# Dealing pooling out ahead of the projection of retention's q and k between the steps of attention

## The chip, the cores and the metric

The kernel runs on one core of a Trainium2 chip. The metric is the device time of one execution in microseconds (us). Engines are named as the profile names them: PE multiplies matrices, ACT applies functions and copies, DVE works elementwise, POOL and SP mainly issue transfers here.

## What is computed

A backbone of two layers over 256 noisy tokens `x` and 256 context tokens `ctx`, width 1024, in fp32. Each layer mixes tokens by three parallel groups of heads that share one input and one output projection, and then applies a channel mixer (a dense SwiGLU in layer 0, the best 2 of 8 experts in layer 1). Only `x` is returned, so layer 1 needs the context only as keys and values.

```python
def token_mixers(hx, hc, w_in, w_out, ...):
    aqx, akx, avx, rqx, rkx, rvx, rgx, ppx = _split_projection(hx @ w_in)
    aqc, akc, avc, rqc, rkc, rvc, rgc, ppc = _split_projection(hc @ w_in)
    ...
    attn_x = _merge_attn(_blocked_attention(qx, k_all, v_all))       # softmax attention, 8 heads
    ...
    ret_x = _ret_output(ret_x, rgx)                                  # retention, 4 heads: rq, rk, rv, gate rg
    pool_x = multiscale_pool(ppx, pool_w, pool_scale)                # means over windows of pp, then pool_w
    mx = jnp.concatenate([attn_x.astype(hx.dtype), ret_x.astype(hx.dtype), pool_x], axis=-1) @ w_out
```

Retention needs rq and rk of the input projection (called q/k below); pooling needs only pp.

## The kernel before

**Products.** An fp32 product is made of three matmuls of rounded parts (`mm3`, L231 to L233: high by high, high by low, low by high). `split` (L161, L162) makes the parts: ACT copies the high part, DVE subtracts it to get the low one. Weights come in blocks of 1 MB through a ring of four (`wload`, L169) and are split the same way. Normalised tokens stand in `hh` and `hl` (`features`), one buffer each.

**PSUM.** Three kinds of buffers: four named `mm` for projections, three named `at` for attention and retention, one named `md`.

**Attention.** `attend` goes over pairs of heads and, within a head, over tiles of 128 queries: four tiles in layer 0 (two of `x` against 512 keys, two of `ctx` against 256), two in layer 1. A tile takes an `at` buffer for its scores (L720, two matmuls), DVE finds the negated maximum (L723), ACT takes the exponential with its sum (L726), DVE inverts and scales (L727, L728), PE transposes (L731, into the same buffer) and ACT copies to SBUF (L734). Only then is the buffer free. After the two heads of a pair, L743 multiplies by the values into another `at` buffer, and that is split into `mixa`. The steps are 4 to prepare and 32 tiles in layer 0, 4 and 16 in layer 1.

**Side work.** `weave` deals out steps of a second generator between the steps of attention, 0.55 of a step for each in layer 0 and one in layer 1. The second generator is a chain: `values` (the projection of retention's v), `gp` (of its gate and of pooling's input), `project_qk` (of its q and k: 32 products of three matmuls, with 512 columns in layer 0 and 256 or 512 in layer 1), and `pool_tokens`. What is left when attention is through its steps is emitted behind it by `finish`.

`project_qk` ends with conversions: POOL clears (L769), ACT copies (L770 to L772) and DVE subtracts (L777). They write into the one buffer of `hh` and `hl` that the projection's matmuls read, so they start only behind the last of those. `pool_tokens` multiplies by the table `band` (L817, 8 matmuls for each of two steps), copies (L821, ACT), multiplies by the pooling weights (L823), scales (L826, DVE) and splits (L161, L162).

**Order.** The program order is not yet that of the engines: a scheduler orders the instructions of each engine from the program order, data dependences and free buffers. The order is fixed when the kernel is built, and each engine keeps to its own.

**Behind it.** `retain` takes scores (L895, from the conversions), masks them (L897) and multiplies by v (L917). The output projection multiplies `w_out` by `mixa`, retention's `mr` and pooling's `mp`, with four `mm` buffers for its sums. In layer 0 POOL also loads the residual (L847).

Of the kernel before, what the change touches and what calls it, by code (L numbers as in the profile page):

```python
# [86 lines left out]
def weave(main, side, ratio):  # L87

    due = 0.0
    for _ in main:  # L90
        due += ratio
        while due >= 1:
            due -= 1
            next(side, None)


class Net:
# [36 lines left out]
    def s2(self, shape, name, dt=F32):  # L134
        return self.tmp.tile(shape, dt, name=name, tag="s2", bufs=5)
# [439 lines left out]
    def mixer(self, l, pool, xin=None):  # L575
# [17 lines left out]
        def tok(cols, n, tiles, evac, ahead=None, tail=1):  # L593

            out = {t: self.mm() for t in tiles}

            def op(o, t, k, wh, wl, start, stop):
                s = slice(t * 128, t * 128 + 128)
                self.mm3(o[:, :n], (hh[:, k, s], hl[:, k, s]), (wh, wl), start, stop)

            yield from self.product(self.units(I["w_in"][l, cols // 256:(cols + n) // 256], n, pace=rate * 512 // n, ahead=ahead), out, op, tail)
            for t in tiles:
                evac(t, out[t])
# [149 lines left out]
        def project_qk():  # L753
            out = {b: self.mm() for b in range(4)}

            def op_qk(o, b, k, wh, wl, start, stop):
                n = QN if b < 2 else 512
                s = slice(b * 128, b * 128 + 128)
                self.mm3(o[:, :n], (wh[:, s], wl[:, s]), (hh[:, k, :n], hl[:, k, :n]), start, stop)

            yield from self.product(self.units(I["w_in"][l, 3:5], 512, pace=rate), out, op_qk, 1)
            qq, kk = self.features()
            qd, qz, kp = qq[:, 0:4, :QN], qq[:, 4:8, :QN], kk[:, 0:4]
            ret.update(qd=qd, qz=qz, kp=kp, kk=kk)
            parts = []
            for hd in range(4):
                i, j = slice(64 * (hd % 2), 64 * (hd % 2) + 64), slice(64 - 64 * (hd % 2), 128 - 64 * (hd % 2))
                q, k = out[hd // 2][i, :QN], out[2 + hd // 2][i]
                nc.gpsimd.memset(qz[j, hd].bitcast(F32), 0.0)  # L769
                nc.scalar.activation(qd[i, hd], q, AF.Copy)  # L770
                nc.scalar.activation(qd[j, hd], q, AF.Copy)
                nc.scalar.activation(kp[i, hd], k, AF.Copy)  # L772
                parts.append((qz[i, hd], q, qd[i, hd]))
                parts.append((kp[j, hd], k, kp[i, hd]))
                if hd % 2:
                    for lo, x, hi in parts:
                        v.tensor_sub(lo, x, hi.bitcast(F32))  # L777
                    parts = []
# [11 lines left out]
        def values():  # L790
            yield from tok(1280, 256, (0, 1, 2, 3), lambda t, p: nc.scalar.activation(rv[:, t], p[:, :256], AF.Copy))

            r3 = rv.rearrange("p t (h d) -> p (t h) d", d=64)
            mu = self.small.tile([128, 16], F32, name="mu", tag="mu", bufs=1)
            v.tensor_reduce(mu, r3, axis=AX.X, op=OP.add)
            v.tensor_scalar(mu, mu, 1.0 / 64, None, op0=OP.mult)
            v.tensor_tensor(r3, r3, mu[:, :, None].to_broadcast([128, 16, 64]), op=OP.subtract)


        def pool_tokens():  # L800
            band, ys = [], []
            for m in range(2):
                t = pool.tile([128, 4, 256], F32, name="band", tag="band", bufs=2)
                nc.sync.dma_start(t, I["band"][:, m * 1024:(m + 1) * 1024].rearrange("p (g t) -> p g t", g=4))
                band.append(t)
            wp = pool.tile([128, 2, 128], F32, name="wp")
            v.memset(wp, 0.0)
            for g in range(4):
                i = 64 * (g % 2)
                nc.gpsimd.dma_start(wp[i:i + 64, g // 2, i:i + 64], I["pool_w"][l, g])  # L810
            for pr in range(2):
                p = self.mm()
                for side in range(QN // 256):
                    for m in range(2):
                        for i in range(2):
                            g = 2 * pr + i
                            nc.tensor.matmul(p[64 * i:64 * i + 64, side * 256:side * 256 + 256],  # L817
                                             lhsT=pp[:, 2 * side + m, g * 64:g * 64 + 64], rhs=band[m][:, g],
                                             start=m == 0, stop=m == 1, tile_position=(0, 64 * i))
                mx = s2([128, 512], "mixed")  # L820
                nc.scalar.activation(mx[:, :QN], p[:, :QN], AF.Copy)  # L821
                p2 = self.mm()
                nc.tensor.matmul(p2[:, :QN], lhsT=wp[:, pr], rhs=mx[:, :QN], start=True, stop=True)  # L823
                y = s2([128, 512], "pooled")
                c = 32 + 2 * l + pr
                v.tensor_scalar(y[:, :QN], p2[:, :QN], self.fcol[:, c:c + 1], None, op0=OP.mult)  # L826
                ys.append(y)
                yield
            mp.extend(pool.tile([128, 2, QN], F32R, name="mp", tag="band", bufs=2) for _ in range(2))
            for pr in range(2):  # L830
                self.split(mp[0][:, pr], mp[1][:, pr], ys[pr][:, :QN])

        mr, mp = [], []
        gp = tok(1536, 512, QT, ev_gp)
        side = chain(*(values(), gp, project_qk(), pool_tokens()))
        weave(attend(), side, 0.55 if need else 1.0)
        finish(side)
        self.mid = self.latest(DVE, ACT)
# [126 lines left out]
        if need:  # L965
            side = self.product(self.units(w[0:2], 512, back=True, pace=1), outs, op_out, 1)
        else:
            side = self.product(self.units(w, 1024, pace=1, order=(0, 2, 6, 4)), outs, op_out, 2)
# [786 lines left out]
```

## Time and profile before

| | |
|---|---|
| median of 3 runs | 1526.49 us (1525.47 to 1529.04) |
| the profiled execution | 1525.96 us, of which 1523.7 us are the span |
| mean granted clock of PE | 0.982 |
| PE | 1453.4 us busy, 95% of the span |
| DVE, ACT | 823.5 us (54%), 617.2 us (41%) |
| POOL | 61.0 us (4%) |
| transfers | 410.82 MB, mean 270 GB/s |

The profile shows one execution. The span runs from the first to the last instruction; 2.3 us of the execution's time lie outside it. Attention's last tiles and the start of the output projection stand at about 185 to 201 us in layer 0 and at 736 to 747 us in layer 1. In each row of a timeline stand the start, the duration, the engine, the line, the output and the inputs, and in brackets how long the engine had been idle and what released it. Matmuls overlap in the pipeline, so durations of neighbours overlap too, and a row of the trace may count one matmul of 64 rows twice.

### The profile page before, as it was taken

What the parts mean: (1) busy time and instruction counts of PE and PEld (TensorE: products, weight loads), DVE (VectorE), ACT (ScalarE), POOL (GpSimd) and SP (SyncE); (2) the same over time, 40 slices, a digit from 0 to 9 for tenths busy, and PEclk for the clock granted to TensorE, in tenths of its full rate; (3) what the DMA queues carried; (4) which work ended last, traced back from release to release, by engine and by line L of the source; (5) the groups of instructions that cost most, each with busy time, mean ns of one, the idle gap of its engine ahead of it and who ended that gap; (6) DMA issues with size and microseconds to landing.
All of it is one profiled execution on the core that took longest, in us unless ns stands there. A gap on an engine that the chain in (4) does not pass through costs nothing. (4 is left out here: it accounts for less than half of the span.)

```text
span 1523.7 us, 22762 instructions
## 1 busy us (share of the span) xinstructions
PE 1453.4 (95%) x9006; PEld 1053.9 (69%) x9007; DVE 823.5 (54%) x1557; ACT 617.2 (41%) x983; POOL 61.0 (4%) x96
## 2 busy tenths in 40 slices
PE   7999999999999999999999999999999899999796
PEld 5777667988878888787666478755786476774462
DVE  3496687774555544877763089515982143533112
ACT  4337654423222222456642177414771243433111
POOL 1010200000000001000000000000001000000000
PEclk9999999999999999999999999999999999999998
DMA  9773223353453625352367999999999999899983
GB/s 348 276 285 138 90 93 138 125 210 122 165 198 123 219 92 199 126 175 91 139 235 310 420 410 420 420 420 420 408 420 414 408 420 408 333 335 349 376 351 158
DMA packets 63044, 410.82 MB, mean 270 GB/s; under 512 B 9477, under 2 KB 10185, under 8 KB 15697
## 3 DMA queue, kind: packets, MB, share of 16 engines
q1 hardware_dynamic: 54864, 392.19, 65.6%
q0 software_dynamic: 5664, 16.29, 3.0%
q8 instruction: 73, 1.20, 0.3%
q10 hardware_dynamic: 2400, 0.79, 0.2%
q14 instruction: 43, 0.34, 0.1%
HBM read 402.27 MB, written 6.98 MB: 269 GB/s over the span
## 5 line engine op out<-in xcount | busy, mean ns | idle before, releaser
L162 DVE TENSOR_TENSOR wl<-w,wh 128x1024 fp32r<-128x1024 f32 x310 | 374.6, 1223 | 256.9 <-ACT wh L161 247.4
L161 ACT ACTIVATE wh<-w 128x1024 fp32r<-128x1024 f32 x310 | 324.0, 1059 | 369.7 <-PE at L233 113.1
L1339 PE MATMUL mm<-w,few 128*64 128x256 f32 (+2 forms) x2624 | 235.0, 346 | 0.0
L1339 PEld LDWEIGHTS mm<-w,few 128*64 128x64 f32 (+1 forms) x2624 | 153.4, 132 | 72.1 <-issue 17.1
L1368 PE MATMUL mm<-w,few 128*64 128x512 f32 (+1 forms) x616 | 111.2, 536 | 0.0
L231 PE MATMUL mm<-hh,wh 128*128 128x512 f32 (+1 forms) x256 | 95.7, 374 | 1.2 <-ACT hh L161 1.2
L232 PE MATMUL mm<-hl,wh 128*128 128x512 f32 (+1 forms) x256 | 95.7, 374 | 0.0
L233 PE MATMUL mm<-hh,wl 128*128 128x512 f32 (+1 forms) x256 | 95.4, 373 | 0.0
L1303 DVE TENSOR_TENSOR mg<-mg,mm 128x256 f32<-128x256 f32 (+2 forms) x36 | 13.6, 378 | 133.7 <-ACT mg L1302 133.7
L1368 PEld LDWEIGHTS mm<-w,few 128*64 128x64 f32 (+1 forms) x616 | 34.9, 129 | 70.7 <-issue 68.9
L233 PE MATMUL mm<-wh,hl 128*128 128x256 f32 (+1 forms) x240 | 80.8, 342 | 0.0
L232 PE MATMUL mm<-wl,hh 128*128 128x256 f32 (+1 forms) x224 | 75.4, 339 | 1.8 <-DVE wl L162 1.8
L231 PE MATMUL mm<-wh,hh 128*128 128x256 f32 (+1 forms) x224 | 75.1, 340 | 0.0
L1302 ACT ACTIVATE mg<-mm 128x256 f32<-128x256 f32 (+3 forms) x54 | 22.8, 422 | 122.2 <-PE mm L1339 84.1
L363 DVE SCALAR_TENSOR_TENSOR wsum<-w,sc,wsum 128x1024 f32<-128x1024 f32 x48 | 59.6, 1280 | 22.9 <-DMA w<-in_w_mod_dram 22.8
L232 PE MATMUL at<-hl,wh 128*128 128x512 f32 (+1 forms) x192 | 71.3, 371 | 0.0
L233 PE MATMUL at<-hh,wl 128*128 128x512 f32 (+1 forms) x192 | 71.3, 371 | 0.0
L231 PE MATMUL at<-hh,wh 128*128 128x512 f32 (+1 forms) x192 | 71.3, 371 | 0.0
L231 PE MATMUL mm<-wh,xh 128*128 128x512 f32 (+1 forms) x144 | 57.9, 402 | 7.5 <-ACT wh L161 7.5
L232 PE MATMUL mm<-wl,xh 128*128 128x512 f32 (+1 forms) x144 | 57.1, 396 | 2.6 <-DVE wl L162 2.6
L231 PEld LDWEIGHTS mm<-hh,wh 128*128 128x128 f32 x256 | 48.2, 188 | 11.2 <-issue 2.1
L233 PE MATMUL mm<-wh,xl 128*128 128x512 f32 (+1 forms) x144 | 55.7, 387 | 0.0
(486 smaller groups left out, 2589.5 us busy)
## 6 DMA issues: line engine op xcount, KB each, us to landing
w<-in_moe_w_dram SPq DMA_DIRECT2D x264, 1024.0 KB, 14.9
w<-in_w_mod_dram SPq DMA_DIRECT2D x48, 1024.0 KB, 4.9
w<-in_ffn_w_dram SPq DMA_DIRECT2D x33, 1024.0 KB, 4.9
w<-in_w_in_dram SPq DMA_DIRECT2D x16, 1024.0 KB, 5.1
w<-in_w_out_dram SPq DMA_DIRECT2D x8, 1024.0 KB, 4.8
gate<-gscr POOLq DMA_DIRECT2D x5, 512.0 KB, 4.6
band<-in_band_dram SPq DMA_DIRECT2D x4, 512.0 KB, 7.4
yrows<-zero POOLq DMA_DIRECT2D x4, 512.0 KB, 7.8
```

The source lines that it names most:

```text
L161: self.nc.scalar.activation(hi, x, AF.Copy)
L162: self.nc.vector.tensor_sub(lo, x, hi.bitcast(F32))
L231: mm(out, lhsT=a[0], rhs=b[0], start=start, stop=False)
L232: mm(out, lhsT=a[0], rhs=b[1], start=False, stop=False)
L233: mm(out, lhsT=a[1], rhs=b[0], start=False, stop=stop)
L363: nc.vector.scalar_tensor_tensor(x, y, c, x, op0=OP.mult, op1=OP.add)
L1302: nc.scalar.activation(s1[:r, :c], h1[:r, :c], AF.Silu)
L1303: v.tensor_mul(s1[:r, :c], s1[:r, :c], h3[:r, :c])
L1339: nc.tensor.matmul(h[i][m * j:m * j + m, :c], lhsT=x[0][:, k], rhs=t[:, k - k0, j * c:j * c + c], start=k == 0, stop=k == KB - 1, tile_pos ...
L1368: nc.tensor.matmul(y[0][m * q:m * q + m, :c], lhsT=x[0][:, b], rhs=w[:, j, c * q:c * q + c], start=f + j == 0, stop=f + j == FB - 1, tile_ ...
```

## The change

In the chain of side work, `pool_tokens` stands ahead of `project_qk`. Nothing is added or removed.

```diff
         gp = tok(1536, 512, QT, ev_gp)
-        side = chain(*(values(), gp, project_qk(), pool_tokens()))
+        side = chain(*(values(), gp, pool_tokens(), project_qk()))
         weave(attend(), side, 0.55 if need else 1.0)
         finish(side)
```

PE, layer 0, behind the last products of `gp` (the first row below, at about 129 us in the trace before); rows with - are of the kernel before, rows with + of the changed one. `mm<-hh,wh` and its like are products of q/k, `mm<-band,pp` pooling, `at` attention.

```order
 L233 MATMUL mm<-wh,hl 128x512
-L231 MATMUL mm<-hh,wh 128x512
+L817 MATMUL mm<-band,pp 64x256
 L731 MATMUL at<-cst,pe 128x128 x8
 L720 MATMUL at<-kT,qT 128x256 x2
-L232 MATMUL mm<-hl,wh 128x512
-L233 MATMUL mm<-hh,wl 128x512
-L231 MATMUL mm<-hh,wh 128x512
+L817 MATMUL mm<-band,pp 64x256 x2
 L720 MATMUL at<-kT,qT 128x256 x2
-L232 MATMUL mm<-hl,wh 128x512
+L817 MATMUL mm<-band,pp 64x256 x2
```

Where one to three matmuls of q/k stood between attention's instructions, one or two of pooling stand now. The first product of q/k now comes behind 18 tiles' scores (36 of L720), 56 transposes (L731), 27 of L743, all 18 of pooling's matmuls and 12 of the modulation for the next sub-layer (L369, L382); the modulation's stand early in that stretch, 8 of L817 with them, and the other 8 of L817 with both of L823 at its end. From the last L382 to the first L823 there are only tiles: 13 of them get scores, and 34 of L731 and 15 of L743 stand there. In layer 1 the like stretch holds 6 tiles' scores, 32 of L731, 16 of L743 and pooling's 10.

PE, layer 0, at the end of the q/k projection, before:

```order
L233 MATMUL mm<-hh,wl 128x512
L720 MATMUL at<-kT,qT 128x256 x2
L731 MATMUL at<-cst,pe 128x128 x6
L743 MATMUL at<-pT,vt 64x256 x5
L731 MATMUL at<-cst,pe 128x128 x2
L743 MATMUL at<-pT,vt 64x256 x3
L743 MATMUL at<-pTc,vt 64x256 x4
L895 MATMUL at<-hh,hl 128x256 x6
L817 MATMUL mm<-band,pp 64x256 x8
L895 MATMUL at<-hh,hl 128x256 x6
L823 MATMUL mm<-mixed,wp 128x512
L817 MATMUL mm<-band,pp 64x256 x8
```

and in the changed kernel:

```order
L232 MATMUL mm<-hl,wh 128x512
L731 MATMUL at<-cst,pe 128x128 x2
L233 MATMUL mm<-hh,wl 128x512
L743 MATMUL at<-pTc,vt 64x256 x3
L895 MATMUL at<-hh,hl 128x256 x12
L231 MATMUL mm<-wh,mixa_775 128x512
L232 MATMUL mm<-wl,mixa_775 128x512
L233 MATMUL mm<-wh,mixa_776 128x512
```

Before, attention's last tiles and all of pooling stood between the last product of q/k (L233) and the output projection, whose first matmul, L231 of `mixa`, follows the second L823 behind the last row here; now three matmuls of L743 and the scores of retention's first head do. The rest of attention's last eight tiles stands among the products of q/k.

ACT, layer 0, in the changed kernel, from the first conversion of q/k on (hh and hl are retention's q and k here):

```order
L772 ACTIVATE hl<-mm 64x512
L734 ACTIVATE pTc<-at 128x2x128
L770 ACTIVATE hh<-mm 64x512
L771 ACTIVATE hh<-mm 64x512
L161 ACTIVATE mixa_775<-at 128x512
L770 ACTIVATE hh<-mm 64x512
L771 ACTIVATE hh<-mm 64x512
L772 ACTIVATE hl<-mm 64x512
```

These are L772, L770 and L771 of retention's first two heads, with one copy of attention (L734) and the split of attention's last pair (L161) among them. The order of SP is the same in both kernels; on POOL the four clears (L769) now stand behind the four loads of the residual (L847) instead of ahead of them. In layer 1, three transposed tiles and eight matmuls of L743 now stand between the last product of q/k and the output projection, and pooling no longer does.

## Rows read from the trace of the kernel before

**Rows 1.** The page, part 1: busy time of each engine over the span

```profile
PE 1453.4 (95%) x9006; PEld 1053.9 (69%) x9007; DVE 823.5 (54%) x1557; ACT 617.2 (41%) x983; POOL 61.0 (4%) x96
```

**Rows 2.** Windows of four stretches: layer 0's two, then layer 1's two

```profile
core 0: us, PE busy (x) PEld busy (x) DVE busy (x) ACT busy (x) POOL busy (x), PEclk, DMA share, GB/s
136.60:169.00 32.40, 32.40 (x179) 21.42 (x179) 20.42 (x54) 19.93 (x50) 3.28 (x6) 1.00 0.28 100
185.90:201.40 15.50, 13.14 (x83) 7.25 (x83) 11.75 (x23) 14.66 (x29) 4.43 (x8) 1.00 0.36 135
700.80:722.40 21.60, 21.60 (x134) 16.55 (x132) 14.00 (x30) 16.63 (x32) 0.00 (x0) 1.00 0.28 98
735.90:747.00 11.10, 8.39 (x39) 4.46 (x38) 9.23 (x18) 10.19 (x24) 1.23 (x4) 0.85 0.70 275
```

**Rows 3.** Windows of 4 us at the ends of the two stretches, columns as above

```profile
184.00:188.00 4.00, 3.40 (x20) 2.23 (x18) 3.22 (x9) 3.43 (x9) 1.82 (x4) 1.00 0.00 0
736.00:740.00 4.00, 2.11 (x11) 1.30 (x9) 2.70 (x6) 3.88 (x10) 1.23 (x4) 1.00 0.21 35
740.00:744.00 4.00, 3.66 (x15) 1.80 (x16) 3.59 (x6) 3.87 (x9) 0.00 (x0) 0.66 0.99 412
744.00:748.00 4.00, 3.52 (x17) 2.16 (x18) 3.92 (x10) 2.73 (x7) 0.00 (x0) 0.91 0.81 342
```

**Rows 4.** Timeline, 120.7 to 125 us: a 512-key tile; start, duration, engine, line

```profile
120.76 1.30 PE L720 MATMUL at<-kT,qT 128*128 128x512 f32 x6
121.41 1.62 DVE L723 TENSOR_REDUCE mx<-at 128x1 f32<-128x512 f32 x3 [0.43 <-PE at L720]
...
122.14 0.69 ACT L726 ACTIVATE pe<-at,mx 128x512 f32<-128x512 f32 x1 [1.58 <-DVE mx L723]
...
123.15 0.49 DVE L728 TENSOR_SCALAR pe<-pe,sm 128x512 f32<-128x512 f32 x1
...
123.78 0.63 PE L731 MATMUL at<-cst,pe 128*128 128x128 f32 x4
...
124.45 0.62 ACT L734 ACTIVATE pT<-at 128x512 f32<-128x512 f32 x1
```

**Rows 5.** Timeline, 180.3 to 184 us: a 256-key tile from scores to copy

```profile
180.47 1.10 PE L720 MATMUL at<-kT,qT 128*128 128x256 f32 x4
...
183.35 0.38 ACT L734 ACTIVATE pTc<-at 128x256 f32<-128x256 f32 x1 [0.24 <-PE at L731]
```

**Rows 6.** Timeline of PE, 184.8 to 202 us: layer 0, end of the q/k projection

```profile
185.26 0.39 PE L232 MATMUL mm<-hl,wh 128*128 128x512 f32 x1
185.49 0.40 PE L233 MATMUL mm<-hh,wl 128*128 128x512 f32 x1
185.87 0.50 PE L720 MATMUL at<-kT,qT 128*128 128x256 f32 x2
...
193.35 1.95 PE L817 MATMUL mm<-band,pp 128*64 128x256 f32 x16
...
196.67 1.12 PE L823 MATMUL mm<-mixed,wp 128*128 128x512 f32 x2 [0.47 <-ACT mixed L821]
...
200.46 1.12 PE L823 MATMUL mm<-mixed,wp 128*128 128x512 f32 x2 [0.78 <-ACT mixed L821]
201.02 0.80 PE L231 MATMUL mm<-wh,mixa 128*128 128x512 f32 x1
```

**Rows 7.** Timeline of ACT, 185 to 194 us: conversions after the projection in layer 0

```profile
187.35 0.59 ACT L772 ACTIVATE hl<-mm 64x512 fp32r<-64x512 f32 x1
...
188.32 0.37 ACT L734 ACTIVATE pTc<-at 128x256 f32<-128x256 f32 x1
...
192.55 0.60 ACT L161 ACTIVATE mixa<-at 128x512 fp32r<-128x512 f32 x1
```

**Rows 8.** Timeline of DVE, 185 to 198 us: the first subtraction after them

```profile
190.39 0.68 DVE L777 TENSOR_TENSOR hh<-mm,hh 64x512 fp32r<-64x512 f32 x1 [0.67 <-ACT hh L771]
```

**Rows 9.** Timeline of PE, 735 to 748 us: layer 1, end of the q/k projection

```profile
740.02 0.65 PE L817 MATMUL mm<-band,pp 128*64 128x256 f32 x2 [1.92 <-DVE hh L777]
```

## The prediction, made before the result was known

> **What bounds the kernel now.** I read the page first: PE is busy for 1453.4 of 1523.7 us [rows 1], so what PE loses or gains at one place shows in the total unless a transfer bounds the part behind it. The rest of the mixer and the dense layer behind it are PE's, so I carry differences through one to one. Next come the windows. While products of q/k stand between attention's instructions, PE does not idle at all (32.40 of 32.40 us, 21.60 of 21.60), though DVE and ACT are busy for only 60 to 80% [rows 2]: one tile's softmax is long, and the products fill the time. At the end of each mixer's attention, where that cover is used up, PE idles: 15.50 less 13.14 is 2.4 us in layer 0, 11.10 less 8.39 is 2.7 us in layer 1, and there the granted clock is 0.85 too, worth 11.1 x 0.15 = 1.7 us [rows 2]. The third view is the timeline of a tile: how long it holds its `at` buffer, of which there are three. The reader is to see that the change lets pooling, a small piece of work, stand between most of attention, and leaves q/k, the big piece, to its end.
>
> **The change, part by part.** Nothing is added. PE's own work stays, apart from how often it changes between kinds. So four things count: the idle time of attention where q/k is gone, the idle time at the new end of each mixer, the clock behind a long gap, and what the old ends lost.
>
> *Layer 0, attention with little cover.* In the order, the bare piece from the last L382 to the first L823 holds 13 tiles' scores (7 of 512 keys, 6 of 256; 26 of L720), 34 of L731 and 15 of L743. At 1.10/4 = 0.27 us each for L720 [rows 5], 0.63/4 = 0.16 for L731 [rows 4], and 0.24 for L743 (by L817, which has its shape, and of which 8 matmuls, counted as 16 in the row, take 1.95 us [rows 6]) this is 7.0 + 5.4 + 3.6 = 16.0 us of PE. The buffers need longer. A tile of 512 keys holds one from 120.76 to the end of its copy at 125.07, 4.3 us; one of 256 keys from 180.47 to 183.73, 3.3 us [rows 4, 5]. A pair's sum holds one for about 6.5 us by my estimate, since its last matmuls stand behind the pair's last tile (3.3) and it then has 12 matmuls (2.9) and a copy. Together 7 x 4.3 + 6 x 3.3 + 6.5 = 56.4 us of buffer, 18.8 us with three: 2.8 us idle if all three are always in use. If the three tiles go in step instead, the third one's exponential waits for two others (2 x 0.69 [rows 4]), a round takes 5.7 us, and 13 tiles take 24.7: 8.7 us idle. I take 5, below the middle, because the nearest row, the end of layer 0's attention with some cover left, has PE busy for 3.40 of 4 us [rows 3], 15% idle, which lies nearer the lower end. Bounds 2.8 and 8.7. Around the bare piece pooling and the modulation give cover, and I count nothing there.
>
> *Layer 0, the new end.* The conversions write what the last product reads, so they start behind it in both kernels. Before, attention's last tiles and pooling covered them. Now PE has three of L743, and then retention's scores, which wait for seven instructions of ACT as the order has them (0.59 + 0.37 + 0.59 + 0.59 + 0.60 + 0.59 + 0.59 = 3.9 us [rows 7]; L770 and L771 have L772's shape) and two of DVE (2 x 0.68 [rows 8]): 5.3 us, less 0.7 for L743, so 4.6 us idle. Bounds: 3 if some of it starts on the last product but one, 5.5 with hand-overs. The four clears on POOL also wait for the last product and stand beside ACT's chain; the residual's loads, now ahead of them, need attention's last scores only, which come earlier. The order of SP doesn't change, so no load moves.
>
> *Clock.* The trace shows what a gap of this size does: in the 4 us from 736 PE was busy for 2.11, with 1.92 us in one piece [rows 9], and then the granted clock was 0.66 for 4 us and 0.91 for the next four [rows 3]; part of that time thus stood at the lower level, 1.2 GHz. That is 4 x 0.34 + 4 x 0.09 = 1.7 us. I take it once for each new end. Bounds 0 and twice that.
>
> *What the old ends lost.* Layer 0's 2.4 us go. Before, L823 waited 0.47 and 0.78 us for ACT behind pooling's copies [rows 6]; among the tiles this wait has other work behind it. A change of kind on PE also costs something: from L233 to L720 it takes 0.38 us, from one product's matmul to the next 0.23 [rows 6]. The order has 93 such changes from `gp`'s last product to the output projection before, 82 now: 11 x 0.15 = 1.6 us less. Bounds 0 and 2.
>
> Layer 0: 5.0 + 4.6 + 1.7 - 2.4 - 1.6 = +7.3 us.
>
> *Layer 1.* The piece without q/k holds 12 of L720, 32 of L731, 16 of L743, 8 of L817 and two short L823 (half of 1.12 us each, for half the columns [rows 6]): 3.2 + 5.1 + 3.8 + 1.9 + 1.1 = 15.1 us of PE. Three tiles hold the buffers at its start; six tiles and two sums follow, 6 x 4.3 + 2 x 6.5 = 38.8, with three buffers 12.9 us, behind a rest of up to 4.3 us: 13 to 17 us. In step it would be some 20. So 0 to 5 us idle; I take 2.5. At its end, ACT has behind the last product and ahead of attention's last copy two exponentials (0.69 and about 0.2 for the sum), two copies (0.62), two of L772 (0.59) and four of L770 and L771 (0.38, as a copy of 256 columns [rows 5]): 5.8 us, and that copy, 6.4. PE has 2 L720 and 12 L731 in that time, 2.5 us: 3.9 idle. Bounds 2 and 5. Gone are 2.7 us of idle time and 1.7 of clock; one new drop is 1.7.
>
> Layer 1: 2.5 + 3.9 + 1.7 - 2.7 - 1.7 = +3.7 us.
>
> **Sum:** +11.0 us on the profiled execution's 1525.96, so **1537.0 us**. That execution lies 0.5 us below the median of the three runs.
>
> One row and one rule differ over the uncovered piece. By the row of 184 to 188 us, PE at 3.40 of 4 us kept a granted clock of 1.00 [rows 3], and so do I for the piece. The Trainium skill, page "TensorE: Matmul & The Clock Gate", section "A second HAM failure mode: psum-queue depth-cycling", says that PE, cycling through PSUM buffers, idles briefly between groups of matmuls so often that its clock swings between the levels, and loses there. By that rule the sum would be the third rival's below; by the row it stays as it is.
>
> **Rivals.** *Nothing idles in the middle.* Three buffers are used as densely as 18.8 us against 16.0 allows, and PE is late into the bare piece, with tiles already through. Then only the ends count: 4.6 + 1.7 + 3.9 + 1.7 - 8.4 = +3.5, 1529.5 us (8.4 is the sum of what goes: 2.4 + 1.6 + 2.7 + 1.7). For it speaks that ACT has only 19.93 of 32.40 us to do [rows 2]; against it, that PE keeps to a fixed order and a tile that is late holds those behind it.
>
> *Faster: the ends close.* If, besides, retention's first scores waited for their own head's three copies and two subtractions alone (3 x 0.59 + 1.36 - 0.7 = 2.4 us), layer 1's end lost only its lower bound (2.0), and neither gap was long enough to lower the clock, the sum would be 2.4 + 2.0 - 8.4 = -4.0, 1522.0 us. It decides from the point where all new losses together stay under 8.4 us. For it: the two old ends were the only places at which PE idled here, and pooling's waits leave both. Against it: the first subtraction before waited for L771 [rows 8], three copies behind its own, and the order shows no work for that gap.
>
> *The clock swings in the middle.* For it: behind a gap of 1.92 us the clock fell [rows 3, 9], and the 5 us of idle time in the bare piece could come in pieces of that size. Against it: gaps of 0.47 and 0.78 us at layer 0's old end left it at 1.00 [rows 2, 6], and three tiles in turn should give small gaps. Each fall costs 1.7 us, as above, and takes 8 us with the recovery; the two pieces, 21 and 17.6 us, hold four at most. With three: 5.2 more, 1542.2 us.
>
> That the change does nothing is excluded, since the order of PE differs in both layers.
>
> **How the numbers follow.** Forecast 0.62, no idle time in the middle 0.14, faster 0.08, clock 0.16. A measurement of this kernel can tell about 0.2% from no change, 3.1 us. Faster by more: nearly all of the faster rival, 0.07. Within it: half of the rival without idle time, the rest of the faster one, and the forecast's lowest values, 0.13. Slower: 0.80. The forecast's own bounds give about 1530 to 1543; the range takes in most of the rival without idle time below and most of the clock's above, 1528.5 to 1544.5, and leaves out the faster one and the ends of the other two, under 0.2.
>
> **What would show it.** In the profile of the changed kernel, the windows of attention in layer 0 (from about 129 us on, some 35 us) should show PE with gaps of 0.3 to 1 us ahead of L731 and L720, released by DVE and ACT, 3 to 9 us in all, at a clock of 1.00; then a stretch of q/k at full occupation; then one gap of 4 to 5 us ahead of the first L895, released by DVE's L777, and a lower clock behind it. Layer 1 should show 0 to 5 us of gaps ahead of q/k, and about 4 us between its last product and the output projection. Pooling's rows should stand among the tiles with no wait of their own. I am wrong if PE is full in the bare piece, if the gap ahead of L895 is under 2 us, or if the dense layer takes back what the mixer lost.

## The result, and the profile after

| | before | changed |
|---|---|---|
| median | 1525.98 us, of the runs beside it (1523.23 to 1529.04) | 1547.33 us, 4 runs (1545.12 to 1548.62) |
| ratio | | 1.0149, 95% interval 1.0127 to 1.0171 |
| span of the profiled execution | 1523.7 us | 1545.8 us |

The changed kernel is 21 us slower; the forecast was 11, with 18.5 as the highest loss in its range. The sign was right and the size was not.

I cut both traces at the same pieces of work. *Mixer 0* goes from the start of `gp`'s last product to that of the last product in the first half of layer 0's `w_out`; *dense* from there to `gp`'s last product in layer 1; *mixer 1* from there to the first product of the expert layer; *experts* is the rest. Where a kernel deals out the two halves of `w_out` in another order, mixer 0 ends where PE has done as many matmuls as before (at the start of the 601st), so that each stretch holds the same work. The wait for q/k is the part of a mixer from `gp`'s last product to the first product of q/k. In us:

| kernel | wait 0 | mixer 0 | dense | wait 1 | mixer 1 | experts | time against before |
|---|---|---|---|---|---|---|---|
| before | 0.2 | 110.6 | 461.1 | 0.2 | 105.0 | 718.2 | |
| changed | 46.0 | 126.8 | 461.1 | 25.2 | 112.4 | 716.3 | 1.0149 [1.0127, 1.0171] |

So layer 0 lost 16.2 us and layer 1 7.4, the dense layer took nothing back, and the experts were 1.9 shorter, which is less than they differ between kernels whose edits leave them alone (715.4 to 721.3 us, below). PE's busy time rose by only 8.2 us; by the page of the changed kernel:

```profile
PE 1461.6 (95%) x9006; PEld 1056.4 (68%) x9007; DVE 824.0 (53%) x1557; ACT 618.5 (40%) x983; POOL 61.0 (4%) x96
```

The instructions are those of [rows 1], so the rest is waiting. The windows of the changed kernel, columns as in [rows 2]: both mixers whole, then the stretch without q/k in layer 0, with the forecast's bare piece and five windows in it, then the new end of layer 0, the stretch without q/k in layer 1 with one window in it, and layer 1's new end.

```profile
129.20:256.00 126.80, 114.93 (x602) 77.99 (x601) 76.35 (x169) 65.33 (x135) 9.66 (x18) 0.95 0.22 77
717.10:829.50 112.40, 100.72 (x567) 69.37 (x565) 70.53 (x184) 61.46 (x125) 1.98 (x5) 0.98 0.39 145
129.40:175.10 45.70, 38.50 (x203) 21.31 (x203) 24.32 (x64) 26.91 (x63) 4.39 (x8) 0.89 0.14 48
139.60:166.80 27.20, 20.17 (x96) 12.80 (x97) 15.72 (x43) 14.64 (x39) 4.39 (x8) 0.84 0.15 59
144.00:148.00 4.00, 2.01 (x11) 1.48 (x12) 2.61 (x8) 2.61 (x8) 1.64 (x3) 0.99 0.06 10
148.00:152.00 4.00, 2.86 (x9) 1.67 (x9) 2.91 (x8) 2.35 (x7) 0.00 (x0) 0.50 0.01 2
152.00:156.00 4.00, 3.74 (x21) 2.72 (x19) 1.36 (x4) 1.65 (x4) 0.00 (x0) 0.65 0.00 0
160.00:164.00 4.00, 2.43 (x14) 1.64 (x14) 3.60 (x9) 2.43 (x6) 0.00 (x0) 1.00 0.00 0
164.00:168.00 4.00, 3.55 (x11) 2.06 (x9) 1.68 (x4) 2.59 (x7) 0.00 (x0) 0.63 0.00 0
216.00:220.00 4.00, 4.00 (x17) 3.56 (x16) 3.83 (x6) 3.94 (x6) 0.00 (x0) 0.57 0.00 0
716.90:742.30 25.40, 19.30 (x100) 10.31 (x99) 12.87 (x31) 16.23 (x35) 0.00 (x0) 0.93 0.12 42
728.00:732.00 4.00, 3.99 (x18) 1.95 (x17) 0.00 (x0) 0.94 (x3) 0.00 (x0) 0.57 0.00 0
767.00:775.60 8.60, 6.00 (x36) 3.52 (x35) 6.66 (x16) 8.28 (x21) 1.43 (x4) 1.00 0.77 297
```

The same two mixers before:

```profile
128.90:239.50 110.60, 107.37 (x602) 74.05 (x601) 75.30 (x169) 64.72 (x135) 9.90 (x18) 1.00 0.25 88
700.60:805.60 105.00, 99.67 (x567) 70.72 (x567) 70.85 (x184) 60.84 (x125) 1.78 (x5) 0.97 0.41 156
```

Idle time of layer 0's mixer went from 110.60 less 107.37 = 3.2 us to 11.9. The clock is next. Counted over busy time it cost 2.86 x 0.50 + 3.74 x 0.35 = 2.7 us in the 8 us from 148 and 3.55 x 0.37 = 1.3 in the 4 from 164, 4.1 unrounded in the stretch without q/k, and 4 x 0.43 = 1.7 at the new end. In the window of 144 us PE is busy for 2.01 of 4 us, and in the next 4 us the clock is 0.50, all of it at the lower level (1.2 GHz); from 160 us on it is busy for 2.43, and the next 4 us have 0.63. Where before a stretch of attention ran at 1.00 and without a gap [rows 2], PE now waits ahead of each round of tiles. Its timeline there, then at layer 0's new end:

```profile
146.42 0.86 PE L731 MATMUL at<-cst,pe 128*128 128x128 f32 x6 [1.40 <-DVE sm L727]
147.74 1.91 PE L720 MATMUL at<-kT,qT 128*128 128x512 f32 x4 [0.45 <-ACT pT L734]
150.78 1.68 PE L731 MATMUL at<-cst,pe 128*128 128x128 f32 x6 [1.14 <-DVE sm L727]
...
163.66 0.87 PE L731 MATMUL at<-cst,pe 128*128 128x128 f32 x6 [1.30 <-DVE sm L727]
...
210.62 1.08 PE L743 MATMUL at<-pTc,vt 128*64 128x256 f32 x6 [0.49 <-ACT pTc L734]
215.13 2.02 PE L895 MATMUL at<-hh,hl 128*128 128x256 f32 x12 [3.43 <-DVE hl L777]
```

Scores are issued together, then their transposes wait together for the softmax: the tiles go in step, as the forecast's upper bound had it.

In layer 1 one gap ahead of L731 is the largest. The timeline of PE, then of ACT just before it:

```profile
726.99 1.30 PE L731 MATMUL at<-cst,pe 128*128 128x128 f32 x8 [3.25 <-DVE sm L727]
```

```profile
722.11 1.28 ACT L944 ACT_TABLE_LOAD   x1
723.40 0.63 ACT L944 ACTIVATE sg<-sg 128x512 f32<-128x512 f32 x1
724.05 1.28 ACT L726 ACT_TABLE_LOAD   x1
725.34 0.69 ACT L726 ACTIVATE pe<-at,mx 128x512 f32<-128x512 f32 x1
```

The gate's silu (L944) comes when `gp` is through. With the table loads ahead of it and of the next exponential it keeps ACT for 3.2 us, and all tiles stand behind it. Both kernels have it, but before it lay beside products of q/k.

### The profile page after: what moved, and what is told of

It reads as the page before. It is cut to its first block, busy times and chain, and to the rows that moved or that the text cites. A ratio compares the mean times of both kernels' runs of the same rounds, so it can differ in the third digit from the quotient of the medians.

```text
span 1545.8 us, 22764 instructions
## 1 busy us (share of the span) xinstructions
PE 1461.6 (95%) x9006; PEld 1056.4 (68%) x9007; DVE 824.0 (53%) x1557; ACT 618.5 (40%) x983; POOL 61.0 (4%) x96
## 5 line engine op out<-in xcount | busy, mean ns | idle before, releaser
L161 ACT ACTIVATE wh<-w 128x1024 fp32r<-128x1024 f32 x310 | 323.9, 1059 | 370.4 <-PE at L233 109.5
L231 PE MATMUL mm<-hh,wh 128*128 128x512 f32 (+1 forms) x256 | 95.7, 374 | 1.2 <-ACT hh L161 1.2
L233 PE MATMUL mm<-hh,wl 128*128 128x512 f32 (+1 forms) x256 | 95.0, 371 | 0.0
L233 PE MATMUL mm<-wh,hl 128*128 128x256 f32 (+1 forms) x240 | 80.7, 341 | 0.0
L231 PE MATMUL mm<-wh,hh 128*128 128x256 f32 (+1 forms) x224 | 75.0, 340 | 0.0
L233 PE MATMUL at<-hh,wl 128*128 128x512 f32 (+1 forms) x192 | 71.3, 371 | 0.0
L231 PE MATMUL at<-hh,wh 128*128 128x512 f32 (+1 forms) x192 | 71.2, 371 | 0.0
L231 PE MATMUL mm<-wh,xh 128*128 128x512 f32 (+1 forms) x144 | 57.9, 402 | 7.5 <-ACT wh L161 7.5
L231 PE MATMUL at<-wh,xh 128*128 128x512 f32 (+1 forms) x144 | 55.5, 386 | 0.0
L231 PEld LDWEIGHTS mm<-hh,wh 128*128 128x128 f32 x256 | 48.2, 188 | 10.7 <-issue 1.5
## 6 DMA issues: line engine op xcount, KB each, us to landing
w<-in_moe_w_dram SPq DMA_DIRECT2D x264, 1024.0 KB, 15.5
```

Of the source, the lines that this page charges most:

```text
L161: self.nc.scalar.activation(hi, x, AF.Copy)
L231: mm(out, lhsT=a[0], rhs=b[0], start=start, stop=False)
L233: mm(out, lhsT=a[1], rhs=b[0], start=False, stop=stop)
```

## Experiments

The first eight rows were run to find the cause, the last four to test parts of it. One execution stands behind each trace column; for the ratio the kernels ran several times beside the kernel before, whose runs spread over 1517.1 to 1531.0 us. So the ratio's interval decides on the total, and a column on its own stretch. How far a column can be trusted, stretches show that an edit leaves alone: mixer 0 took 110.6 us in three kernels, mixer 1 103.0 to 105.0, the experts 715.4 to 721.3.

| kernel | wait 0 | mixer 0 | dense | wait 1 | mixer 1 | experts | time against before |
|---|---|---|---|---|---|---|---|
| l0_only | 46.1 | 126.9 | 461.1 | 0.2 | 104.6 | 717.1 | 1.0132 [1.0094, 1.0169] |
| l1_only | 0.2 | 110.6 | 461.1 | 25.1 | 113.9 | 717.5 | 1.0088 [1.0064, 1.0113] |
| before_hop | 0.3 | 117.3 | 461.6 | 0.2 | 104.7 | 718.0 | 1.0048 [1.0031, 1.0066] |
| after_hop | 47.1 | 130.2 | 461.1 | 25.9 | 117.7 | 717.7 | 1.0216 [1.0190, 1.0242] |
| after_own | 18.7 | 113.8 | 461.0 | 18.5 | 111.9 | 716.6 | 1.0083 [1.0057, 1.0109] |
| after_md | 0.2 | 115.0 | 460.5 | 0.2 | 106.5 | 717.4 | 1.0066 [1.0046, 1.0087] |
| before_md | 0.2 | 107.4 | 467.1 | 0.2 | 103.4 | 715.7 | 1.0035 [1.0023, 1.0047] |
| after_spin | 49.1 | 130.5 | 467.3 | 14.2 | 102.9 | 719.6 | 1.0182 [1.0161, 1.0202] |
| after_silu | 41.6 | 123.4 | 460.6 | 23.3 | 110.6 | 717.2 | 1.0108 [1.0082, 1.0133] |
| md_four | 0.2 | 107.4 | 460.6 | 0.2 | 104.9 | 721.3 | 1.0002 [0.9988, 1.0016] |
| md_l1 | 0.2 | 110.6 | 461.0 | 0.2 | 104.9 | 715.4 | 1.0012 [1.0000, 1.0024] |
| md_l0_four | 0.2 | 107.4 | 460.6 | 0.2 | 103.0 | 717.9 | 0.9977 [0.9961, 0.9994] |

**The change in one layer alone.** The edit is shown against the kernel before; `need` is true in layer 0.

```diff
-side = chain(*(values(), gp, project_qk(), pool_tokens()))
+side = chain(*((values(), gp, pool_tokens(), project_qk()) if need
+               else (values(), gp, project_qk(), pool_tokens())))
```

> Pooling goes ahead of q/k in layer 0 alone; layer 1 keeps the order of before. Theory A (cover): without products of q/k between them, attention's tiles leave PE waiting for DVE and ACT, and the granted clock falls behind the gaps; each layer pays for itself. Then this run takes layer 0's share as read from the changed kernel's trace, where layer 0's last product lies 16 us later than before: 16 us over the kernel before, plus or minus 2.5, with the clock below 1.00 between 140 and 170 us and in 4 us behind the gap ahead of the first L895. Rival B (carried on): the shift of layer 0 sets layer 1's transfers off and layer 1 or the experts make part of the loss; then under 12 us here, or over 20.

The other way round, for layer 1:

> Pooling goes ahead of q/k in layer 1 alone. Theory A: layer 1's share, 7.7 us by the start of the experts in the changed kernel's trace and some 2 us less at the end: 5.5 us over the kernel before, plus or minus 2.5. Rival B: layer 1's loss comes from the late start of layer 1 in the changed kernel; then within 2 us of the kernel before.

Layer 0 alone was 17.1 us slower by the medians, 16.3 by its mixer's trace: as expected. Layer 1 alone cost more than expected, 8.9 us by its trace, and 1.0088 by the clock of the runs (9.8 to 17.2 us); what the runs have beyond the trace stands in no stretch, and I leave it open. That layer 1 needs layer 0's change to lose is false.

**A longer chain per tile.** A link on POOL between L727 and L728:

```diff
+nc.gpsimd.tensor_scalar(sm, sm, 1.0, None, op0=OP.mult)
```

> The kernel before with one more link in each tile's chain: POOL multiplies the reciprocal sum by 1.0 between L727 and L728 (48 tiles; the result is the same; DVE, ACT and PE get no more work). Theory A: products of q/k cover it; 0 to 3 us over the kernel before, from the ends where the cover is gone. Rival C (fixed order, not the chain: PE loses because its order is a bad one): the same small cost here and in the changed kernel.

> The changed kernel with the same link. Theory A: a link of 0.7 to 1.0 us lengthens each stay in one of three buffers; 18 tiles in layer 0 and 8 in layer 1 have no cover, 26 x 0.85 / 3 = 7 us, and more where the clock falls: 5 to 12 us over the changed kernel, and clearly more than what the link costs the kernel before. Rival C: the same as in the kernel before, 0 to 3 us.

Expected was that a covered attention would not feel the link and an uncovered one would. But the kernel before lost some 7 us too, and the changed one some 10 by the ratios, each known to a few us only, so the pair does not tell the theories apart. The link was also shorter than the 0.7 to 1.0 us expected: POOL's instruction takes 0.21 us, and DVE's multiplication (L728 before) starts 0.40 us behind L727 where it started 0.04 behind it (medians of the 48 tiles). The loss before was not in the covered stretch alone (59.0 us from the first to the last product of q/k, 56.4 without the link) but still more at attention's end (19.9 us from there to `w_out`, 15.5 without it). Windows of before_hop:

```profile
188.00:192.00 4.00, 2.03 (x12) 1.22 (x11) 2.42 (x8) 3.28 (x9) 2.54 (x6) 0.95 0.02 4
192.00:196.00 4.00, 3.74 (x18) 2.50 (x18) 2.58 (x8) 3.23 (x8) 1.88 (x4) 0.50 0.15 19
196.00:200.00 4.00, 4.00 (x20) 1.85 (x20) 2.48 (x5) 2.47 (x7) 0.74 (x2) 0.70 0.91 364
```

There the clock falls as it does in the changed kernel. Also the scheduler gave another order with the link in it, so this experiment changed more than a length.

**Why q/k comes so late.** q/k sums into all four `mm` buffers; pooling's two sums are in `mm` as well, and such a buffer is free only when ACT has copied it to `mixed` (L821). `mixed` and `pooled` come from a ring of five buffers that attention's `pe` and `pTc` use too, and it is handed out in program order. So the copy stands behind 13 tiles. One kernel gives the two tiles buffers of their own, the other puts the sums in the buffer `md`:

```diff
-mx = s2([128, 512], "mixed")
+mx = self.tmp.tile([128, 512], F32, name="mixed", tag="own", bufs=2)
...
-y = s2([128, 512], "pooled")
+y = self.tmp.tile([128, 512], F32, name="pooled", tag="own", bufs=2)
```

> The changed kernel, with two SBUF buffers of its own for pooling's copies mixed and pooled, which otherwise come from the ring of five that attention's tiles use (name s2). Theory E (held banks): in the changed kernel the ring hands its buffers out in program order, so ACT's L821 stands behind 13 more tiles; until then pooling holds mm banks, and q/k, which wants all four, cannot start. Then here q/k starts about 4 tiles behind gp, the bare piece is gone with its 7 us of idle time and 5 us of clock in layer 0 and the like in layer 1, and only the new ends stay: 0 to 6 us over the kernel before, some 16 to 21 us under the changed kernel. Theory A alone (cover goes whenever pooling stands among the tiles): within 6 us of the changed kernel.

```diff
-p = self.mm()
+p = self.md()
...
-p2 = self.mm()
+p2 = self.md()
```

> The changed kernel, with pooling's sums in the one md bank of PSUM in place of mm banks; its copies stay in the shared ring. Theory E: pooling is as late as in the changed kernel, but holds nothing that q/k wants, so q/k starts right behind gp: 0 to 6 us over the kernel before. If the ring of copies itself were what costs (rival F), the time would stay within 6 us of the changed kernel's.

The copy in ACT's timeline of the changed kernel, then with buffers of their own; last the first product of q/k there, on PE:

```profile
165.53 0.61 ACT L821 ACTIVATE mixed<-mm 128x512 f32<-128x512 f32 x1
```

```profile
135.86 0.59 ACT L821 ACTIVATE mixed<-mm 128x512 f32<-128x512 f32 x1
```

```profile
147.71 0.48 PE L231 MATMUL mm<-hh,wh 128*128 128x512 f32 x1
```

In the changed kernel the product waited for it, and for the second copy at 172.99, until 175.12. With its own buffers layer 0 loses 3.2 us instead of 16.2, with `md` 4.4: the cause of most of layer 0's loss is shown. That pooling and q/k share buffers costs 12 to 13 us of the 16.2, and the order of the chain the rest. But the kernel before pays for the shared buffers too: with `md` in both orders (before_md below) the mixers take 115.0 us against 107.4 and 106.5 against 103.4, so there the order costs 7.6 and 3.1. Layer 1 lost 6.9 and 1.5: with own buffers q/k still comes behind the silu, and its gap is there unchanged (3.25 us at 713.78, released by L727); with `md` q/k starts at once and covers it. The totals missed: 12.6 and 10.0 us, where 0 to 6 was expected, and the traces have 10.1 and 5.3 in mixers and dense layer.

What is left with `md` in layer 0 is the new end that the forecast described; the window of its mixer, then PE's timeline at that end:

```profile
126.10:241.15 115.05, 110.36 (x601) 75.21 (x600) 76.33 (x170) 66.31 (x138) 9.67 (x18) 0.99 0.25 88
...
199.83 3.61 PE L895 MATMUL at<-hh,hl 128*128 128x256 f32 x16 [4.03 <-DVE hl L777]
```

**The same edit on the kernel before.** There pooling's wait for buffers ends each mixer, so `md` should be a gain.

> The kernel before, with pooling's sums in the md bank: at the end of the mixer pooling then needs no bank that q/k's conversions still hold, and can stand in their gap. Expected by the gaps of the kernel before: 1 to 2 us less in layer 0 and 2 to 4 us less in layer 1 (1.9 us of idle time ahead of L817 and 1.7 us of clock), so 2 to 6 us under the kernel before. If the conversions' gap on ACT and DVE sets the end anyway, within 2 us of it.

The mixers gained, 3.2 and 1.6 us, but the dense layer lost 6.0, and the time rose. The second half of `w_out` sums into three `at` buffers and `md`; its products for `md` now came early and did not cover the postnorm. PE's timeline and a window:

```profile
261.71 0.46 PE L547 MATMUL at<-diag,res 128*128 128x128 f32 x2 [3.99 <-DVE rsq_t L151]
```

```profile
260.00:264.00 4.00, 2.25 (x11) 2.09 (x12) 2.52 (x20) 1.34 (x4) 0.00 (x0) 0.80 1.01 337
```

**Filling the gaps.** A matmul of no use in each tile of the first two pairs, to hold the clock:

```diff
+if pr < 2:
+    self.spin(self.md(), 1, 256)
 yield
```

> The changed kernel, with one idle matmul on PE (128x256, into the md bank, used by nobody) behind each tile of the first two pairs of heads in each layer, 24 in all, some 0.4 us each, about 10 us of work. Theory G (the clock is a loss of its own): the granted clock stays near 1.00 in the bare piece, where it was 0.75 to 0.83, and the matmuls fall into idle time: 2 to 7 us under the changed kernel. Rival H (the gaps alone count, and what runs slowly runs beside waits anyway): the same time or up to 8 us more.

The clock stayed up, and there was less idle time; the time did not fall. Layer 0's stretch without q/k:

```profile
129.80:178.60 48.80, 45.00 (x234) 24.82 (x234) 24.17 (x64) 26.92 (x63) 4.57 (x8) 0.97 0.12 45
```

48.8 us at 0.97 stand against 45.7 at 0.89: 10.7 us of matmuls were added and the stretch grew by 3.1, so they filled gaps and slow time, but cost more than they gave. In layer 1, where some of them stand ahead of `gp`'s end, dense and mixer together went from 573.5 to 570.2 us. Over the mixers and the dense layer the traces thus differ by 0.4 us only; most of the rest of the profiled loss, 3.3 us, stands in the experts, which the edit leaves alone.

**The silu out of the way.** On ACT, behind attention's instructions:

```diff
-nc.scalar.activation(sg, sg, AF.Silu)
+with self.behind(self.latest(ACT)):
+    nc.scalar.activation(sg, sg, AF.Silu)
```

> The changed kernel, with the gate's silu (L944, two activation table loads and one activation, 3.2 us of ACT by the rows at 722 us) put behind attention's instructions on ACT instead of straight behind gp. Theory S (in layer 1 the gap of 3.25 us ahead of L731, released by L727, and the fall of the clock behind it come from this silu, which q/k's products cover in the kernel before): that gap shrinks below 1.5 us, the stretch from gp's last product to the first product of q/k in layer 1 falls from 25.2 to 20-22.5 us, layer 0's stays within 1 us of 46.0, and the time falls by 2 to 6 us against the changed kernel. Rival (the gap is that of the tiles' own chain, and the table loads only happen to stand in it): the stretch stays within 1 us of 25.2, and the time within 2 us.

The gap of 3.25 us is gone, and the largest in its place is 1.41, by L821. The time fell by 6 us against the changed kernel (1.0149 to 1.0108). But layer 1's mixer gave only 1.8 of them; layer 0's gave 3.4, where I had expected none. There the silu and its two loads stood on ACT from 131.91 to 135.56 us. Layer 0's mixer without them, then the stretch without q/k in layer 0 and in layer 1:

```profile
128.75:252.20 123.45, 114.48 (x602) 76.67 (x601) 76.92 (x170) 67.06 (x138) 9.94 (x18) 0.96 0.23 81
129.00:170.70 41.70, 37.47 (x204) 19.36 (x203) 23.80 (x64) 23.27 (x60) 4.63 (x8) 0.96 0.15 52
712.80:736.20 23.40, 19.32 (x100) 10.82 (x99) 12.72 (x30) 13.26 (x31) 0.00 (x0) 0.93 0.13 46
```

Layer 0 has 4.2 us idle in that stretch in place of 7.2, at 0.96 in place of 0.89. Some of its matmuls also stand in another order there, so whether the silu's place or that order did it is not shown.

**A version that beats both.** `md` for pooling in the kernel before, and the sums of `w_out`'s second half in another order, so that an `at` group comes last (both in md_four; md_l1 has `md` in layer 1 alone):

```diff
-return [self.at(), self.at(), self.at(), self.md()]
+return [self.md(), self.at(), self.at(), self.at()]
```

> The kernel before, with pooling's two sums in the buffer md instead of two mm buffers, and with the four sums of w_out's second half taken in the order md, at, at, at instead of at, at, at, md. The run before_md had won 3.2 us in layer 0's mixer and 1.6 in layer 1's by the trace and lost 6.0 in the dense layer, by a gap of 4 us ahead of L547 and a low clock behind it, since w_out's md products came early and covered the postnorm no longer. Theory (that loss is only the order of the four): the gap ahead of L547 is under 1 us again, the dense stretch is within 1.5 us of 461.1, the mixers keep 3 to 5 us together, and the time is 2 to 5 us under the kernel before. Rival (any product that leaves the end of w_out uncovers the postnorm): the dense stretch still takes 464 us or more, and the time is no lower than the kernel before's.

> The kernel before, with pooling's two sums in md in layer 1 alone. Theory (with its own PSUM buffer pooling no longer waits for q/k's sums at layer 1's end): the stretch from gp to the first expert product takes 103 to 104 us instead of 105.0, layer 0 and the dense layer are within 0.5 us of the kernel before, and the time is 0 to 2.5 us lower. Rival (the conversions are what ends last there): no change within 1 us.

The dense layer is whole again in md_four (460.6; from 260 to 268 us the clock is 1.00 and PE busy for 7.21 us, 6.78 in the kernel before), so the loss in before_md was the order of the four. Layer 0 keeps its 3.2 us. Layer 1 does not: by md_l1, `w_out` starts 7.3 us sooner behind q/k and is through no sooner, since PE waits in it now, as on retention's output:

```profile
771.29 0.41 PE L951 MATMUL at<-cst,ro 128*128 128x128 f32 x2 [1.96 <-DVE ro L946]
```

Neither was faster; md_four's experts took 3.1 us more in its trace, which I cannot explain. So the last kernel has `md` in layer 0 alone, with the new order of the four:

> The kernel before, with pooling's two sums in md in layer 0 alone, and the four sums of w_out's second half in the order md, at, at, at. In the run md_four layer 0's mixer took 3.2 us less and the dense layer 0.5 less by the trace, while layer 1 won 7.3 us ahead of w_out and lost 7.2 behind it. Theory (each mixer has its own balance: in layer 0 the freed wait stays a gain, in layer 1 what pooling covered behind the mixer opens again): layer 0's mixer at 107.4 us, the dense stretch at 460 to 461.5, layer 1 at 105.0 within 0.5, together 3 to 4 us under the kernel before in the part up to the expert layer, and the time 1 to 4.5 us lower. Rival (the expert layer, with transfers at 1.01 of their share in most of its windows, takes an earlier start back): the part up to it is 3 to 4 us shorter, the expert layer as much longer, and the time within 1 us of the kernel before.

Its median is 1519.63 us against 1524.50 beside it, ratio 0.9977 [0.9961, 0.9994]: the one kernel of the study that is faster than the kernel before, by 0.2% and with an interval that ends close to 1. Its mixer 0 has no idle time left:

```profile
126.20:233.60 107.40, 107.28 (x601) 73.84 (x600) 74.11 (x166) 64.88 (x135) 9.87 (x18) 1.00 0.25 89
```

Layer 1 took 103.0 and not 105.0, at a clock of 1.00 where the kernel before had 0.97, though the edit leaves it alone; that part I do not count as the edit's.

## Why the prediction was wrong in size

**The idle time of layer 0 was about right.** Forecast: 5.0 in the middle, 4.6 at the new end, 2.4 gone, +7.2. Measured: +8.6 for the whole mixer, with 7.2 in the middle, 7.0 of it in the bare piece (bounds 2.8 and 8.7), and 3.9 at the end (3.43 and 0.49); the two errors go opposite ways and partly cancel.

**The failed step is the clock of the middle.** "By the row of 184 to 188 us, PE at 3.40 of 4 us kept a granted clock of 1.00 [rows 3], and so do I for the piece" was wrong: the clock fell in the windows from 148 and 164 us in layer 0, for 4.1 us, and in that from 728 in layer 1, for 1.7. The row was idle for 15% of its time, while the piece was forecast at 5 of 21 us, 24%, and came to 7.0 of 27.2, 26%. And tiles in step made that uneven: PE was busy for 2.01 of the 4 us at 144 and for 2.43 of those at 160, and behind each the clock fell. The fault was to carry the clock of a row over to a piece with more idle time, in larger lumps. The third rival had this mechanism, its number and its price: three falls, 5.2 us, against 5.8 measured. I had given that rival a chance of 0.16. The Trainium skill, page "TensorE: Matmul & The Clock Gate", section "A second HAM failure mode: psum-queue depth-cycling", has the rule that PE, idling briefly between groups as it cycles through PSUM, swings between the two levels; the trace agrees, at 0.89 over the stretch.

**Clock at the new end:** 1.7 taken, 1.7 measured in layer 0. **Changes of kind on PE:** 1.6 taken as a gain, not seen. Busy time less what the clock cost is 107.4 before and 114.9 - 4.1 - 1.7 = 109.1 after, 1.7 more. Part of it is pooling's first product: L817 alone keeps PE for 3.89 us in layer 0's mixer before, in two blocks, and for 6.01 in the changed kernel, a few at a time among the tiles (overlap with neighbours included). The rest I have not resolved. So layer 0 is the forecast's 7.3, and 1.4 of idle time, 4.1 of clock and 3.3 of busy time over it: 16.1, measured 16.2.

**Layer 1's middle** was forecast at 2.5 us of idle time and 1.00. It has 25.40 less 19.30 = 6.1, above the bound of 5, besides the fall of the clock. The step that failed counted `at` buffers per tile and left out what else stands on ACT behind `gp`: the silu and its two loads, 3.2 us, which the row of ACT's busy share in [rows 2] held without naming. The new end was better than forecast: 2.6 us idle, where 3.9 was taken, and no fall of the clock where 1.7 was. With these differences 3.7 becomes 3.7 + 3.6 + 1.7 - 1.3 - 1.7 = 6.0 us; the mixer lost 7.4, and the other 1.4 I cannot place.

**The ends alone** show the same missing gain. With `md`, q/k starts at once and the ends are what is left of the loss: +4.4 and +1.5 us by the mixers. The forecast's terms without its middles give 4.6 + 1.7 - 2.4 - 1.6 = 2.3 and 3.9 + 1.7 - 2.7 - 1.7 = 1.2. Layer 1's is near; layer 0's would be 3.9 without the 1.6 for changes of kind, and there too PE's busy time rose, by 3.0 us (110.36 against 107.37), some of it the clock's fall at the end, while the idle time rose by 1.5.

**Not in the forecast at all:** why the piece without q/k is that long. I took its length from the order and asked only what it holds. That pooling's copy waits for a buffer of a ring shared with attention is what turns 3 to 4 us into 16.

## What to carry over

Ahead of moving a small step in front of a large one, ask which buffers the small one still holds while it waits, and whether the large one needs them: a copy that waits for a shared ring can hold up another engine's main work. Where a stretch loses its cover, list all of each engine's instructions in it, not the tiles' alone, and look at how its idle time is bunched, and at the clock behind each bunch, not at the mean alone.

## What was not expected of the hardware

- No single gap of the changed kernel around 146 us is over 1.40 us, and yet the clock was 0.50 for the next 4 us; at layer 0's end a gap of 3.43 us was followed by 0.57 and then 1.00. Several small gaps together lowered it as one large one did.
- A table load takes 1.28 us, and the next instruction starts within 0.02 us behind it (723.40 behind 722.11 + 1.28). One silu among exponentials costs two of them, four times its own 0.63 us. The Trainium skill, page "ScalarE: Activation LUTs", section "What ACT_TABLE_LOAD costs", states 1283 ns, which the rows show, and a drain of some 1380 ns beside it, which they don't show here.
- Added matmuls can hold the clock up (0.97 in place of 0.89) and still bring nothing: with 10.7 us of them the stretch without q/k was 3.1 us longer.
